# Dealing a modulation's partial sums out between weight splits, and joining the sample's statistics in one matmul

## Chip, cores and metric

One core of a Trainium2 chip runs the whole program. The metric is device time in microseconds: the median of 3 runs, beside one profiled execution, from which every duration below is taken. Engines: TensorE (PE), VectorE (DVE), ScalarE (ACT), GpSimd (POOL), and SyncE (SP), whose queue issues the loads of the weights.

## What is computed

One layer of a streaming encoder, in fp32, for 256 prompt and 32 sample tokens (288 columns) of width 2048:

```python
mod = jax.nn.silu(c) @ w_ada + b_ada
sh1, sc1, g1, sh2, sc2, g2 = [t[:, None, :] for t in jnp.split(mod, 6, axis=-1)]
u = layer_norm(x) * (1 + sc1) + sh1
t, pool_state, C, n, m = token_mixer(u, ...)
x = layer_norm(ALPHA * x + g1 * t, ln1_g, ln1_b)
u = layer_norm(x) * (1 + sc2) + sh2
f = (jax.nn.silu(u @ w_gate) * (u @ w_up)) @ w_down
x = layer_norm(ALPHA * x + g2 * f, ln2_g, ln2_b)
```

`token_mixer` projects u by w_in (2048 x 13328), pools one part over windows, runs 8 heads of mLSTM attention with carried state on another, and merges both by w_pa, w_pb and w_out. `mod` has six parts of 2048, for prompt and sample: j = 0 and 1 feed the first norm, j = 2 to 5 (the later modulation) are needed after w_out.

## The kernel before

All weights are streamed once, in units of 512 KB (128 x 1024 fp32). TensorE multiplies in a split form: the weight is cast to a high part on ACT (L97), the rest of it is taken on DVE as a low part (L98), and each k-tile and block of 128 columns takes three products of 288 columns: hi x hi (L199), hi x lo of the activations (L200), lo of the weight x hi (L201). A full unit makes 24 such matmuls. There are 579 weight units and 192 units of w_ada; the latter are "plain", with no split. 64 of these go to TensorE (parts 0 and 1), and 128 to DVE: the later modulation consists of 16 sums (j, c), each over 8 units, and `ada_dve` issues four steps for a unit (two k-tiles by prompt and sample, L335 and L337), each adding 128 x 512 scaled weights to `aacc`. After the eighth unit a small background task (`ada_sum`) joins the partitions with 8 matmuls, adds the bias and sets `modF`.

The class `Weights` sets the order of the streaming. `_loads` (L79 to L87) issues loads on SP into a ring of `RAW_BUFS = 6` buffers: up to six units ahead of `done`, the oldest plain unit that is converted and not yet used, or else the number of converted units. `_split` issues cast and lo into a ring of four hi/lo pairs. `next` is called as the program takes up a unit; it converts ahead until `depth` weight units are ready (2, then 4), then hands out its own. The program is scheduled by hand: the order in which instructions are written is the order on each engine.

The plan runs: setup and a staged start while parts 0 and 1 of the modulation are made; then groups of 256 output columns, four units each (`group`): w_in for heads 2 to 7, in the order v, o, k, q (24 groups, `rest`), the gates with w_pa and w_pb (`merge`), w_out, then the second norm, w_gate and w_up in pairs, w_down. After each group comes `ada_slot`, which takes as many ada units as a quota has become due: 96 of the 128 in `rest`, merge and w_out by the weights `R`, 32 in gate and up (`ADA_LATE`). Within a group `pump` runs small background tasks: attention for the heads (its instructions are around L930 to L1110), evacuations, parts of the sums.

Sample tokens lie on 4 blocks of 32 partitions (4 blocks of 512 columns); `block_stats` (L425 to L440) joins mean and variance of the blocks with two matmuls by `sel4` and four small DVE instructions, at setup, in `norm_open` (second norm, end) and in `second`.

Of the kernel before, what the change touches and what calls it, by code (L numbers as in the profile page):

```python
# [37 lines left out]
GW = 256  # L38
# [11 lines left out]
class Weights:  # L50
# [3 lines left out]
    def __init__(self, nc, raw_p, cv_p):  # L54
        self.nc, self.raw_p, self.cv_p = nc, raw_p, cv_p
        self.units, self.blocks, self.srcs = [], [], None
        self.raw, self.ready = {}, {}
        self.n_dma = self.n_conv = self.pos = 0
        self.depth = 0

    def add(self, name, k0, nk, c0, ncols):

# [15 lines left out]

    def _loads(self):  # L79
        live = [u for u in range(self.pos, self.n_conv) if self.units[u][1]]  # L80
        done = min(live + [self.n_conv])
        while self.n_dma < min(len(self.units), done + RAW_BUFS):
            shape = self.units[self.n_dma][0]
            t = self.raw_p.tile(shape, F32, tag="raw", name="raw", bufs=RAW_BUFS)
            self.nc.sync.dma_start(out=t, in_=self.srcs[self.n_dma])
            self.raw[self.n_dma] = t
            self.n_dma += 1  # L87

    def _split(self, u):
        shape, plain = self.units[u]  # L90
        raw = self.raw.pop(u)
        if plain:
            self.ready[u] = (raw, None, shape[1])
            return
        hi = self.cv_p.tile(shape, F32R, tag="hi", name="hi", bufs=CONV_BUFS)
        lo = self.cv_p.tile(shape, F32R, tag="lo", name="lo", bufs=CONV_BUFS)
        self.nc.scalar.copy(hi, raw)  # L97
        self.nc.vector.tensor_tensor(lo, raw, hi, op=ALU.subtract)  # L98
        self.ready[u] = (hi, lo, shape[1])

    def next(self, keep=0):

        self.ready.pop(self.pos - 1, None)
        self._loads()
        held = sum(not self.units[u][1] for u in range(self.pos - keep, self.n_conv))
        while self.n_conv < self.n_dma and (held < self.depth or self.units[self.n_conv][1]):
            held += not self.units[self.n_conv][1]
            self._split(self.n_conv)
            self.n_conv += 1
            self._loads()  # L110
        self.pos += 1
        return self.ready[self.pos - 1]
# [3 lines left out]
def tile_stream_layer(  # L116
# [15 lines left out]
    dram = ctx.enter_context(tc.tile_pool(name="spill", bufs=1, space=bass.MemoryType.DRAM))  # L132
    kw_d, v_d = (dram.tile([NH, 128, 2, HD], F32, name=n) for n in ("kwd", "vd"))
    W = Weights(nc, raw_p, cv_p)
    plan, bg, pools, T = [], [], {}, {}

    n_misc = [0]

# [180 lines left out]

    def ada_dve(j, c, q):  # L320

        n = CS // 512

        def run():
            raw = W.next()[0]
            if q == 0:
                while T.get("aacc_busy"):
                    run_task(T["aacc_busy"])
                T["aacc"] = small.tile([128, 2, 512], F32, tag="aacc", name="aacc")
            acc = T["aacc"]  # L330
            for kk in range(n):
                for s in range(2):
                    col = scl[:, n * q + kk, s:s + 1]
                    if q == 0 and kk == 0:
                        nc.vector.tensor_scalar(out=acc[:, s], in0=raw[:, kk], scalar1=col, scalar2=None, op0=ALU.mult)  # L335
                    else:
                        nc.vector.scalar_tensor_tensor(out=acc[:, s], in0=raw[:, kk], scalar=col, in1=acc[:, s],  # L337
                                                       op0=ALU.mult, op1=ALU.add)
            if q == KT // n - 1:
                while T.get("sum"):  # L340
                    run_task(T["sum"])
                T["sum"] = T["aacc_busy"] = later(ada_sum(j, c, acc), 4)

        plain((("w_ada", q * n, n, j * D + c * 512, 512), run))

    def ada_end(j, c, t):
        k0 = 4 * c
# [3 lines left out]
    def ada_sum(j, c, acc):  # L351
        t = misc()
        for g in range(4):
            for s in range(2):
                nc.tensor.matmul(t[32 * g:32 * g + 32, 0:128], lhsT=es[:, s], rhs=acc[:, s, g * 128:(g + 1) * 128],  # L355
                                 start=(s == 0), stop=(s == 1), tile_position=(0, 32 * g))
        T["aacc_busy"] = None
        yield from ada_end(j, c, t)
        T["sum"] = None

    dve_left = [(j, c, q) for j, c in ADA_DVE for q in range(8)]

# [59 lines left out]
        for g in gens:  # L422
            yield from g

    def block_stats(mv):  # L425

        mean, v = mv[:, 0:1], mv[:, 1:2]
        t = misc()
        nc.tensor.matmul(t[:, 0:1], lhsT=sel4, rhs=mean, start=True, stop=True)
        yield 1  # L430
        d = small.tile([128, 2], F32, tag="dmv", name="dmv", bufs=2)
        nc.vector.tensor_tensor(d[:, 0:1], mean, t[:, 0:1], op=ALU.subtract)
        nc.vector.scalar_tensor_tensor(out=d[:, 1:2], in0=d[:, 0:1], scalar=d[:, 0:1], in1=v,
                                       op0=ALU.mult, op1=ALU.add)
        nc.vector.tensor_copy(mean, t[:, 0:1])
        t = misc()
        nc.tensor.matmul(t[:, 0:1], lhsT=sel4, rhs=d[:, 1:2], start=True, stop=True)
        yield 1
        nc.vector.tensor_copy(v, t[:, 0:1])
        yield 1  # L440

    def stat_tiles():
        return (small.tile([128, 3, 2], F32, tag="mv", name="mv", bufs=3),
                small.tile([128, 3], F32, tag="rstd", name="rstd", bufs=3))

    def aggr(sts):


        n = len(sts)
        mv, r = stat_tiles()  # L450
        for i, (st, blocks) in enumerate(sts):
            nc.vector.bn_aggr(out=mv[:, i], in_=st)
            if blocks:
                for _ in block_stats(mv[:, i]):
                    pass
        rsqrt(r[:, 0:n], mv[:, 0:n, 1])
        return [(mv[:, i], r[:, i:i + 1]) for i in range(n)]

    def row_stats(src):
        n = src.shape[1] // 512  # L460
        st = small.tile([128, 4, 6], F32, tag="bst", name="bst", bufs=3)[:, 0:n]
        weave(stat_steps(src, st))
        return st, n == 1

    def stat_steps(src, st):
        for c in range(st.shape[1]):
# [105 lines left out]
    cnt = const.tile([128, 16], F32, name="cnt")  # L572
    nc.gpsimd.iota(cnt, pattern=[[1, 16]], base=1, channel_multiplier=0, allow_small_or_imprecise_dtypes=True)
    nc.vector.reciprocal(out=cnt, in_=cnt)
    sel4 = const.tile([128, 128], F32, name="sel4")
    for b in range(1, 4):
        nc.gpsimd.tensor_tensor(sel4[:, 0:32], ident[:, 0:32] if b == 1 else sel4[:, 0:32],
                                ident[:, b * 32:(b + 1) * 32], op=ALU.add)
    nc.gpsimd.tensor_scalar(out=sel4[:, 0:32], in0=sel4[:, 0:32], scalar1=0.25, scalar2=None, op0=ALU.mult)
    nc.gpsimd.tensor_copy(sel4[:, 32:64], sel4[:, 0:32])  # L580
    nc.gpsimd.tensor_copy(sel4[:, 64:128], sel4[:, 0:64])
    es4 = const.tile([128, 2], F32, name="es4")
    nc.gpsimd.tensor_scalar(out=es4, in0=sel4[:, 0:2], scalar1=4.0, scalar2=None, op0=ALU.mult)
    modF = const.tile([128, 6, 16, 2], F32, name="modF")
    vecF = const.tile([128, 120], F32, name="vecF")
    cn = const.tile([128, 48], F32, name="cn")
# [24 lines left out]
    def setup():  # L611
# [28 lines left out]
        for s in range(2):  # L640
            nc.scalar.activation(out=scl[:, :, s], in_=t[:, 16 * s:16 * s + 16], func=AF.Silu)
        x, (mv, r) = T["x"], stat_tiles()
        for i in range(3):
            nc.vector.bn_aggr(out=mv[:, i], in_=row_stats(x[i])[0])
        nc.vector.tensor_copy(cn, t[:, 0:48])

        def rest():
            bs = block_stats(mv[:, 2])
            for _ in range(3):
                yield next(bs)  # L650
            rsqrt(r, mv[:, :, 1])
            for c in (slice(0, 512), slice(512, D)):
                for i in (2, 0, 1) if c.start == 0 else (0, 1):
# [493 lines left out]
        return f  # L1147

    def out_open():
        close_pool("bh")  # L1150
        close_pool("ua")
        p = open_pool("xr", "left")
# [38 lines left out]
    def norm_open(fill):  # L1191

        drain()
        mv, r = T["stat"] = stat_tiles()
        bs = block_stats(mv[:, 2])
        first = chain(*[affine(i, 0, mv, r) for i in range(3)])
        nc.vector.bn_aggr(out=mv[:, 2], in_=T["st"][2])
        next(bs)
        for i in range(2):
            nc.vector.bn_aggr(out=mv[:, i], in_=T["st"][i])  # L1200
        for _ in range(2):
            next(fill, None)
            next(first)
            next(bs)
        weave(rsqrt_steps(r, mv[:, :, 1]), first, fill)

    def second_open():
        T["states"] = state_steps()
        norm_open(every(F[0], islice(T["states"], F[1])))
        close_pool("mg")  # L1210
# [5 lines left out]
    def second():  # L1216
# [21 lines left out]
        def early():  # L1238
# [5 lines left out]
            for c in cs:  # L1244
                norm(0, c)

        weave(chain(affine(0, 1, mv, r), stats(0)), every(F[2], islice(fill, 8 - F[1])),
              chain(affine(2, 1, mv, r), stats(2), block_stats(mv2[:, 2])))
        weave(chain(affine(1, 1, mv, r), stats(1)), twice(early()), every(F[3], fill))
        rsqrt(r2[:, 1:2], mv2[:, 1:2, 1])  # L1250
        sample_columns(T["xs"], xh[2])
# [60 lines left out]
        return keep if part == 0 else res_evac(j, 5, last) if part == NPART - 1 else more  # L1312

    def fin_open():
        close_pool("u2")
        p = open_pool("ln2", "left")
        T["gb"] = row_tiles(p, ("g2", "b2"))
# [29 lines left out]
    merge += [(x, j) for j in range(1, D // GW) for x in "ab "[j == 1:]]  # L1347
    n_ada, n1, n2 = [0], len(dve_left) - ADA_LATE, len(dve_left)
    late = [w for x, j in merge for w in R[1 + (j > 1)][x]] + [R[3]] * (D // GW - 2) + [0, 0]
    quota = chain(shares(n1, [R[0]] * len(rest) + late), (n1 + n for n in shares(n2 - n1, [1] * (2 * (DFF // GW) - 4) + [0] * 4)))  # L1350
    for u in ada_first(0):
        plain(u)
        do(lambda: next(T["setup"]))
# [56 lines left out]
            group("w_down", f0, FPT, j * GW, GW, "act", down_evac(part, j))  # L1410
    do(finish)
    W.bind(pack)
    for step in plan:
        step()

# [48 lines left out]
```

## Time and profile before

| what | us |
|---|---|
| median of 3 runs (lowest, highest) | 2040.82 (2037.26, 2042.93) |
| profiled execution | 2038.8 |
| its span | 2036.9 |
| PE busy | 1972.4 |
| DVE busy | 1381.4 |
| ACT busy | 772.8 |

How to read it: an engine's busy time is the sum of what it worked on, the span runs from the first to the last instruction. A timeline row gives start, duration, engine, line, operation, result <- operands, shape, number of instructions, and in brackets how long the engine had been idle and who released it. A row of waits gives engine, line, who is waited for, us in total, times, the longest. A row of the windows gives the stretch and its length, then each engine's busy time with instructions in it, the granted clock of TensorE (1.00 is full), the share of time of the DMA engines and GB/s. A row of DMA issues gives result <- source, queue, number, KB, and the median us from issue to landing.

### The profile page before, as it was taken

Reading aid. Unit: us, or ns where it says so; the run is one execution under the profiler, and the core shown is the slowest. Engines: PE = TensorE matmul, PEld = TensorE weight load, DVE = VectorE, ACT = ScalarE, POOL = GpSimd, SP = SyncE. Lnnn points to the kernel's source line nnn. Section 1 sums busy time; section 2 is a strip of 40 time slices with the busy share of each in tenths; the row PEclk is TensorE's granted clock in tenths of the full one; section 3 lists DMA queues with packets and bytes.
Section 4 is the critical chain, followed back from the end, with each engine's and each line's share of the span. In section 5 each row is a group of like instructions: output and inputs, shape, how many; then the busy total and the mean of one; then the engine's idle time right before and its main releaser. Section 6 shows DMA issues by size and latency. Waiting matters only on the chain.

```text
span 2036.9 us, 36604 instructions
## 1 busy us (share of the span) xinstructions
PE 1972.4 (97%) x14952; PEld 1898.4 (93%) x14952; DVE 1381.4 (68%) x2341; ACT 772.8 (38%) x1106; POOL 75.1 (4%) x132
## 2 busy tenths in 40 slices
PE   6999999999999999999999899999999999999995
PEld 5788889999999999999999799999999999999995
DVE  6777787888798568877787765656544565565555
ACT  3333444343433433333334453333333333333331
POOL 1000022000001000000000100000000000001000
PEclk9999999999999999999999899999999999999998
DMA  8878657666666557767797356556555566666541
GB/s 288 280 267 269 198 187 225 209 231 210 213 217 214 160 187 237 238 223 234 231 330 252 126 170 196 195 192 207 180 171 167 189 195 195 196 197 209 180 157 61
DMA packets 126040, 421.85 MB, mean 207 GB/s; under 512 B 14302, under 2 KB 23238, under 8 KB 125104
## 3 DMA queue, kind: packets, MB, share of 16 engines
q1 hardware_dynamic: 118320, 405.59, 61.2%
q0 software_dynamic: 2976, 9.18, 1.5%
q10 hardware_dynamic: 4576, 4.74, 0.7%
q8 instruction: 117, 1.92, 0.4%
q14 instruction: 51, 0.42, 0.1%
HBM read 408.57 MB, written 10.89 MB: 206 GB/s over the span
## 4 chain that ended last, share of the span: by engine, by line
PE 88%; DVE 7%; ACT 2%; DMA 2%; issue 1%; DVEq 0%; ACTq 0%
PE acc L199 28%; PE acc L200 27%; PE acc L201 27%; DVE lo L98 2%; DMA raw<-in_w_in_dram 1%; PE ada L303 1%; DVE aacc L337 1%; ACT hi L97 1%; PE m L539 1%; PE m L1040 1%; DVE xt L1187 0%; DVE xt L1184 0%; PE m L355 0%; PE m L1071 0%; DVE pf L706 0%
## 5 line engine op out<-in xcount | busy, mean ns | idle before, releaser
L98 DVE TENSOR_TENSOR lo<-raw,hi 128x1024 fp32r<-128x1024 f32 (+2 forms) x579 | 680.6, 1185 | 492.5 <-ACT hi L97 490.7
L97 ACT CAST hi<-raw 128x1024 fp32r<-128x1024 f32 (+2 forms) x579 | 585.0, 1015 | 753.6 <-PE acc L200 485.0
L199 PE MATMUL acc<-uhi,hi 128*128 128x288 f32 x1680 | 510.3, 304 | 10.1 <-ACT hi L97 5.2
L201 PE MATMUL acc<-uhi,lo 128*128 128x288 f32 x1680 | 497.3, 296 | 6.7 <-DVE lo L98 6.7
L200 PE MATMUL acc<-ulo,hi 128*128 128x288 f32 x1680 | 498.5, 297 | 0.0
L199 PE MATMUL acc<-vhi,hi 128*128 128x288 f32 x1408 | 418.0, 297 | 0.8 <-ACT vhi L474 0.8
L200 PE MATMUL acc<-vlo,hi 128*128 128x288 f32 x1408 | 416.7, 296 | 0.2 <-DVE vlo L475 0.2
L201 PE MATMUL acc<-vhi,lo 128*128 128x288 f32 x1408 | 416.6, 296 | 0.0
L199 PEld LDWEIGHTS acc<-uhi,hi 128*128 128x128 f32 x1680 | 317.8, 189 | 41.3 <-issue 25.2
L337 DVE SCALAR_TENSOR_TENSOR aacc<-raw,scl,aacc 128x512 f32<-128x512 f32 x480 | 328.1, 750 | 0.0
L201 PEld LDWEIGHTS acc<-uhi,lo 128*128 128x128 f32 x1680 | 317.2, 189 | 8.0 <-DVE lo L98 7.8
L200 PEld LDWEIGHTS acc<-ulo,hi 128*128 128x128 f32 x1680 | 317.6, 189 | 0.2
L199 PEld LDWEIGHTS acc<-vhi,hi 128*128 128x128 f32 x1408 | 266.0, 189 | 2.2 <-ACT vhi L474 1.4
L200 PEld LDWEIGHTS acc<-vlo,hi 128*128 128x128 f32 x1408 | 264.9, 188 | 0.7 <-DVE vlo L475 0.6
L201 PEld LDWEIGHTS acc<-vhi,lo 128*128 128x128 f32 x1408 | 265.4, 188 | 0.0
L199 PE MATMUL acc<-acthi,hi 128*128 128x288 f32 x704 | 208.2, 296 | 0.0
L201 PE MATMUL acc<-acthi,lo 128*128 128x288 f32 x704 | 207.8, 295 | 0.0
L200 PE MATMUL acc<-actlo,hi 128*128 128x288 f32 x704 | 207.7, 295 | 0.0
L199 PEld LDWEIGHTS acc<-acthi,hi 128*128 128x128 f32 x704 | 132.4, 188 | 0.2 <-issue 0.2
L201 PEld LDWEIGHTS acc<-acthi,lo 128*128 128x128 f32 x704 | 132.2, 188 | 0.0
L200 PEld LDWEIGHTS acc<-actlo,hi 128*128 128x128 f32 x704 | 132.1, 188 | 0.0
L200 PE MATMUL acc<-blo,hi 128*128 128x288 f32 x256 | 75.9, 296 | 1.1 <-DVE blo L475 1.1
(307 smaller groups left out, 1924.4 us busy)
## 6 DMA issues: line engine op xcount, KB each, us to landing
raw<-in_w_in_dram SPq DMA_DIRECT2D x202, 512.0 KB, 4.4
raw<-in_w_ada_dram SPq DMA_DIRECT2D x192, 512.0 KB, 4.4
raw<-in_w_gate_dram SPq DMA_DIRECT2D x88, 512.0 KB, 4.3
raw<-in_w_up_dram SPq DMA_DIRECT2D x88, 512.0 KB, 3.8
raw<-in_w_down_dram SPq DMA_DIRECT2D x80, 512.0 KB, 3.5
raw<-in_w_pb_dram SPq DMA_DIRECT2D x32, 512.0 KB, 4.5
raw<-in_w_out_dram SPq DMA_DIRECT2D x32, 512.0 KB, 5.4
raw<-in_w_pa_dram SPq DMA_DIRECT2D x16, 512.0 KB, 4.4
```

The lines of the kernel that those rows point to most:

```text
L97: self.nc.scalar.copy(hi, raw)
L98: self.nc.vector.tensor_tensor(lo, raw, hi, op=ALU.subtract)
L199: nc.tensor.matmul(o, lhsT=hi[:, kk, c], rhs=xh[:, k], start=first, stop=False)
L200: nc.tensor.matmul(o, lhsT=hi[:, kk, c], rhs=xl[:, k], start=False, stop=False)
L201: nc.tensor.matmul(o, lhsT=lo[:, kk, c], rhs=xh[:, k], start=False, stop=last)
L303: nc.tensor.matmul(t[q:q + 32, j * w:j * w + w], lhsT=scl[:, r0 + i, :], rhs=raw[:, i], start=(r0 + i < 4), stop=(r0 + i >= KT - 4), tile_ ...
L337: nc.vector.scalar_tensor_tensor(out=acc[:, s], in0=raw[:, kk], scalar=col, in1=acc[:, s], op0=ALU.mult, op1=ALU.add)
L539: nc.tensor.transpose(dst, full[:, t0:t0 + n], ident)
L1040: nc.tensor.matmul(t[0:n, c:c + b - a], lhsT=k[:, dt, s0:s0 + n], rhs=q[:, dt, a:b], start=(dt == 0), stop=(dt == 1))
```

## The change

1. `ada_dve` no longer issues its four steps when its unit is taken up. It queues them in `steps`, and `deal` issues two (more if over eight would stay) after each split (`W.between`). The unit stays in `W.held` until its last step; `_loads` counts six units from the oldest held one. If a unit is taken up that has no load yet, `next` deals until it has. `parts_done` issues all that is left and runs the sums' tasks, at the start of w_out, of the second norm, and of the last w_down.
2. The quota of the first six groups of `rest` falls from 1.9 to 0.8; the other groups get the rest.
3. `join` replaces `block_stats`: the blocks' raw statistics are spread with a mask (`block`) in one DVE multiply, brought to all blocks by one matmul (`same`) and aggregated once.

```diff
     def _loads(self):
         live = [u for u in range(self.pos, self.n_conv) if self.units[u][1]]
-        done = min(live + [self.n_conv])
+        done = min([*live, *self.held, self.n_conv])
         while self.n_dma < min(len(self.units), done + RAW_BUFS):
...
         self.nc.vector.tensor_tensor(lo, raw, hi, op=ALU.subtract)
         self.ready[u] = (hi, lo, shape[1])
+        self.between()
 
     def next(self, keep=0):
 
         self.ready.pop(self.pos - 1, None)
         self._loads()
+        while self.n_dma <= self.pos:
+            self.between()
+            self._loads()
...
+            if (kk, s) != (n - 1, 1):
+                return
+            W.held.discard(u)
             if q == KT // n - 1:
...
         def run():
             raw = W.next()[0]
+            W.held.add(W.pos - 1)
+            for kk in range(n):
+                for s in range(2):
+                    steps.append((raw, W.pos - 1, kk, s, step))
+
         plain((("w_ada", q * n, n, j * D + c * 512, 512), run))
+
+    def deal(n=2):
+
+        for _ in range(min(len(steps), max(n, len(steps) - 8))):
+            *a, step = steps.pop(0)
+            step(*a)
...
+    def parts_done(*js):
+
+        deal(len(steps))
+        while any((j, c) not in T.get("parts", ()) for j in js for c in range(4)):
+            run_task(T["sum"])
...
-    def block_stats(mv):
-
-        mean, v = mv[:, 0:1], mv[:, 1:2]
+    def join(mv, st):
+
+
+        w = st.shape[1] * 6
+        flat = small.tile([128, 2 * NT], F32, tag="tmp", name="join", bufs=TMP_BUFS)[:, 0:4 * w]
+        e = flat.rearrange("p (b c) -> p b c", b=4)
+        nc.vector.tensor_tensor(e, st.rearrange("p (o n) c -> p o (n c)", o=1).to_broadcast([128, 4, w]),
+                                block.rearrange("p (b o) -> p b o", o=1).to_broadcast([128, 4, w]), op=ALU.mult)
         t = misc()
-        nc.tensor.matmul(t[:, 0:1], lhsT=sel4, rhs=mean, start=True, stop=True)
+        nc.tensor.matmul(t[:, 0:4 * w], lhsT=same, rhs=flat, start=True, stop=True)
         yield 1
...
+        nc.vector.bn_aggr(out=mv, in_=t[:, 0:4 * w].rearrange("p (n c) -> p n c", c=6))
         yield 1
...
-    quota = chain(shares(n1, [R[0]] * len(rest) + late), (n1 + n for n in shares(n2 - n1, [1] * (2 * (DFF // GW) - 4) + [0] * 4)))
+    quota = chain(shares(n1, [0.8] * 6 + [R[0]] * (len(rest) - 6) + late), (n1 + n for n in shares(n2 - n1, [1] * (2 * (DFF // GW) - 4) + [0] * 4)))
...
     W.bind(pack)
+    W.between = deal
```

The line numbers move: casts L97 are now L99, lo L98 is L100, the products are L205 to L207, the steps L338 and L340, copies L938 are L946, the state's update L982 is L990.

First place: ACT, in groups of the heads (`pf` are copies of a group's result out of PSUM; `eo`, `kw`, `vT`, `dd` and `b` belong to attention). Before:

```order
L938 COPY pf<-acc 128x288 x2
L97 CAST hi<-raw 128x1024
L1074 COPY dd<-m 32x257
L97 CAST hi<-raw 128x1024 x2
L963 ACTIVATE eo<-m 128x512
L964 ACTIVATE eo<-m 32x256
L97 CAST hi<-raw 128x1024
L974 ACTIVATE kw<-m,wst 128x256 x2
```

Now:

```order
L946 COPY pf<-acc 128x288 x2
L99 CAST hi<-raw 128x1024 x4
L982 ACTIVATE kw<-m,wst 128x256 x2
L982 ACTIVATE kw<-m,wst 32x256
L983 DMA kwd<-kw 128x512
L946 COPY pf<-acc 128x288 x2
L99 CAST hi<-raw 128x1024
L275 COPY adarow<-m 128x128
L99 CAST hi<-raw 128x1024 x3
```

Casts that stood one by one between the attention's instructions now stand in a row behind the copies of the group before.

Second place: DVE, in the same groups (`co` is the state's update from a matmul, `hh` the norm of a head's result). Before:

```order
L471 TENSOR_SCALAR hh<-hh,hmv,hrr 32x256
L98 TENSOR_TENSOR lo<-raw,hi 128x1024 x3
L337 SCALAR_TENSOR_TENSOR aacc<-raw,scl,aacc 128x512 x8
L98 TENSOR_TENSOR lo<-raw,hi 128x1024
L982 SCALAR_TENSOR_TENSOR co<-c_5116,dec,m 128x257 x2
L98 TENSOR_TENSOR lo<-raw,hi 128x1024 x3
L337 SCALAR_TENSOR_TENSOR aacc<-raw,scl,aacc 128x512 x8
```

Now:

```order
L990 SCALAR_TENSOR_TENSOR co<-c_5031,dec,m 128x257 x2
L340 SCALAR_TENSOR_TENSOR aacc<-raw,scl,aacc 128x512 x4
L287 TENSOR_TENSOR modF<-m,vecF 128x4 x2
L289 TENSOR_SCALAR modF<-modF 128x8
L100 TENSOR_TENSOR lo<-raw,hi 128x1024
L338 TENSOR_SCALAR aacc<-raw,scl 128x512 x2
L100 TENSOR_TENSOR lo<-raw,hi 128x1024
L340 SCALAR_TENSOR_TENSOR aacc<-raw,scl,aacc 128x512 x2
L100 TENSOR_TENSOR lo<-raw,hi 128x1024 x2
```

The block of eight steps is gone. The last four steps of a unit, which free its buffer, and the four lo parts of the group that PE takes up next all stand behind the state's update of the group before.

## Rows read from the trace of the kernel before

**Rows 1.** Span and mean granted clock of the core

```profile
core 0: 2036.9 us, clock 0.987
```

**Rows 2.** Busy time of each engine, share of the span, instructions

```profile
PE 1972.4 (97%) x14952; PEld 1898.4 (93%) x14952; DVE 1381.4 (68%) x2341; ACT 772.8 (38%) x1106; POOL 75.1 (4%) x132
```

**Rows 3.** Waits of PE

```profile
PE acc L201 <- DVE lo L98: 6.7, 5, 4.4
...
PE m L200 <- DVE ylo L475: 2.8, 1, 2.8
...
PE m L437 <- DVE dmv L433: 0.9, 1, 0.9
```

**Rows 4.** Timeline of PE around the gap at 291

```profile
291.00 0.29 PE L200 MATMUL acc<-ulo,hi 128*128 128x288 f32 x1
295.68 0.40 PE L201 MATMUL acc<-uhi,lo 128*128 128x288 f32 x1 [4.38 <-DVE lo L98]
```

**Rows 5.** Timeline of DVE in the same place

```profile
287.16 7.33 DVE L337 SCALAR_TENSOR_TENSOR aacc<-raw,scl,aacc 128x512 f32<-128x512 f32 x8
294.42 2.35 DVE L98 TENSOR_TENSOR lo<-raw,hi 128x1024 fp32r<-128x1024 f32 x2
```

**Rows 6.** Windows: one of rows 9, two behind gaps, one without a gap

```profile
core 0: us, PE busy (x) PEld busy (x) DVE busy (x) ACT busy (x) POOL busy (x), PEclk, DMA share, GB/s
201.50:210.19 8.69, 8.28 (x73) 6.77 (x65) 5.54 (x15) 2.36 (x3) 0.00 (x0) 1.00 0.89 336
295.68:299.50 3.82, 3.82 (x18) 3.82 (x19) 3.69 (x8) 1.11 (x2) 0.00 (x0) 0.58 0.83 295
326.60:329.00 2.40, 2.12 (x9) 2.12 (x10) 2.40 (x5) 0.13 (x1) 0.50 (x1) 0.58 0.65 213
1200.00:1250.00 50.00, 50.00 (x379) 50.00 (x378) 29.97 (x36) 19.29 (x24) 0.00 (x0) 1.00 0.60 186
```

**Rows 7.** DMA issues of the weights

```profile
raw<-in_w_in_dram SPq DMA_DIRECT2D x202, 512.0 KB, 4.4
...
raw<-in_w_down_dram SPq DMA_DIRECT2D x80, 512.0 KB, 3.5
...
raw<-in_w_out_dram SPq DMA_DIRECT2D x32, 512.0 KB, 5.4
```

**Rows 8.** Groups of lo and cast: busy us, mean ns of one, idle before, releaser

```profile
L98 DVE TENSOR_TENSOR lo<-raw,hi 128x1024 fp32r<-128x1024 f32 (+2 forms) x579 | 680.6, 1185 | 492.5 <-ACT hi L97 490.7
L97 ACT CAST hi<-raw 128x1024 fp32r<-128x1024 f32 (+2 forms) x579 | 585.0, 1015 | 753.6 <-PE acc L200 485.0
```

**Rows 9.** The critical chain from 195 to 215: start, us, what

```profile
200.89 0.61 PE ada L303 x8
201.52 5.71 DMA raw<-in_w_in_dram
...
207.30 1.06 ACT hi L97
...
208.39 1.23 DVE lo L98
```

**Rows 10.** Waits of SP's queue on the steps

```profile
SPq L85 <- DVE aacc L337: 255.7, 113, 4.3
```

**Rows 11.** Timeline of DVE in a group of the heads

```profile
421.86 5.38 DVE L337 SCALAR_TENSOR_TENSOR aacc<-raw,scl,aacc 128x512 f32<-128x512 f32 x8
...
445.19 0.88 DVE L982 SCALAR_TENSOR_TENSOR co<-c,dec,m 128x257 f32<-128x257 f32 x2
```

**Rows 12.** Timeline of DVE at an evacuation of up

```profile
1189.59 0.46 DVE L1293 TENSOR_TENSOR sg<-sg,acc 128x288 f32<-128x288 f32 x1 [1.57 <-PE acc L201]
...
1192.82 3.50 DVE L98 TENSOR_TENSOR lo<-raw,hi 128x1024 fp32r<-128x1024 f32 x3 [0.49 <-ACT hi L97]
```

**Rows 13.** Timeline of ACT at copies of a group's result

```profile
435.53 0.70 ACT L938 COPY pf<-acc 128x288 f32<-128x288 f32 x2
```

**Rows 14.** Timeline of DVE at the last norm

```profile
2018.26 0.22 DVE L433 SCALAR_TENSOR_TENSOR dmv<-dmv,mv 128x1 f32<-128x1 f32 x1
```

More of the change, by code (lines that the diff above doesn't have):

```diff
@@ L59, in __init__ @@
         self.depth = 0
+        self.held = set()
+        self.between = lambda: None
     def add(self, name, k0, nk, c0, ncols):
@@ L134, in tile_stream_layer @@
     W = Weights(nc, raw_p, cv_p)
-    plan, bg, pools, T = [], [], {}, {}
+    plan, bg, pools, T, steps = [], [], {}, {}, []
     n_misc = [0]
@@ L322, in ada_dve, with step @@
         n = CS // 512
-        def run():
-            raw = W.next()[0]
-            if q == 0:
+        def step(raw, u, kk, s):
+            if q == kk == s == 0:
                 while T.get("aacc_busy"):
@@ L329, in run @@
                 T["aacc"] = small.tile([128, 2, 512], F32, tag="aacc", name="aacc")
[L330 to L338, printed above, removed]
+            acc, col = T["aacc"], scl[:, n * q + kk, s:s + 1]
+            if q == 0 and kk == 0:
+                nc.vector.tensor_scalar(out=acc[:, s], in0=raw[:, kk], scalar1=col, scalar2=None, op0=ALU.mult)
+            else:
+                nc.vector.scalar_tensor_tensor(out=acc[:, s], in0=raw[:, kk], scalar=col, in1=acc[:, s],
+                                               op0=ALU.mult, op1=ALU.add)
+            if (kk, s) != (n - 1, 1):
+                return
+            W.held.discard(u)
             if q == KT // n - 1:
@@ L342, in run @@
                 T["sum"] = T["aacc_busy"] = later(ada_sum(j, c, acc), 4)
+        def run():
+            raw = W.next()[0]
+            W.held.add(W.pos - 1)
+            for kk in range(n):
+                for s in range(2):
+                    steps.append((raw, W.pos - 1, kk, s, step))
         plain((("w_ada", q * n, n, j * D + c * 512, 512), run))
+    def deal(n=2):
+        for _ in range(min(len(steps), max(n, len(steps) - 8))):
+            *a, step = steps.pop(0)
+            step(*a)
     def ada_end(j, c, t):
@@ L359, in ada_sum @@
         T["sum"] = None
+        T["parts"] = T.get("parts", frozenset()) | {(j, c)}
+    def parts_done(*js):
+        deal(len(steps))
+        while any((j, c) not in T.get("parts", ()) for j in js for c in range(4)):
+            run_task(T["sum"])
     dve_left = [(j, c, q) for j, c in ADA_DVE for q in range(8)]
@@ L423, in chain @@
             yield from g
-    def block_stats(mv):
-        mean, v = mv[:, 0:1], mv[:, 1:2]
+    def join(mv, st):
[4 more added lines that the diff above has]
+                                block.rearrange("p (b o) -> p b o", o=1).to_broadcast([128, 4, w]), op=ALU.mult)
         t = misc()
-        nc.tensor.matmul(t[:, 0:1], lhsT=sel4, rhs=mean, start=True, stop=True)
+        nc.tensor.matmul(t[:, 0:4 * w], lhsT=same, rhs=flat, start=True, stop=True)
         yield 1
[L431 to L439, printed above, removed]
+        nc.vector.bn_aggr(out=mv, in_=t[:, 0:4 * w].rearrange("p (n c) -> p n c", c=6))
         yield 1
@@ L444, in stat_tiles @@
                 small.tile([128, 3], F32, tag="rstd", name="rstd", bufs=3))
[L446 to L457, printed above, removed]
     def row_stats(src):
@@ L462, in row_stats @@
         weave(stat_steps(src, st))
-        return st, n == 1
+        return st
     def stat_steps(src, st):
@@ L574, in tile_stream_layer @@
     nc.vector.reciprocal(out=cnt, in_=cnt)
-    sel4 = const.tile([128, 128], F32, name="sel4")
+    same = const.tile([128, 128], F32, name="same")
     for b in range(1, 4):
-        nc.gpsimd.tensor_tensor(sel4[:, 0:32], ident[:, 0:32] if b == 1 else sel4[:, 0:32],
+        nc.gpsimd.tensor_tensor(same[:, 0:32], ident[:, 0:32] if b == 1 else same[:, 0:32],
                                 ident[:, b * 32:(b + 1) * 32], op=ALU.add)
[L579 to L583, printed above, removed]
+    nc.gpsimd.tensor_copy(same[:, 32:64], same[:, 0:32])
+    nc.gpsimd.tensor_copy(same[:, 64:128], same[:, 0:64])
+    es4 = same[:, 0:2]
+    block = const.tile([128, 4], F32, name="block")
+    nc.vector.tensor_reduce(block, ident.rearrange("p (b c) -> p b c", b=4), axis=mybir.AxisListType.X, op=ALU.add)
     modF = const.tile([128, 6, 16, 2], F32, name="modF")
@@ L642, in setup @@
         x, (mv, r) = T["x"], stat_tiles()
-        for i in range(3):
-            nc.vector.bn_aggr(out=mv[:, i], in_=row_stats(x[i])[0])
-        nc.vector.tensor_copy(cn, t[:, 0:48])
+        for i in range(2):
+            nc.vector.bn_aggr(out=mv[:, i], in_=row_stats(x[i]))
         def rest():
-            bs = block_stats(mv[:, 2])
-            for _ in range(3):
-                yield next(bs)
+            yield from join(mv[:, 2], row_stats(x[2]))
+            nc.vector.tensor_copy(cn, t[:, 0:48])
             rsqrt(r, mv[:, :, 1])
@@ L1149, in out_open @@
     def out_open():
+        parts_done(2)
         close_pool("bh")
@@ L1194, in norm_open @@
         mv, r = T["stat"] = stat_tiles()
-        bs = block_stats(mv[:, 2])
+        bs = join(mv[:, 2], T["st"][2])
         first = chain(*[affine(i, 0, mv, r) for i in range(3)])
-        nc.vector.bn_aggr(out=mv[:, 2], in_=T["st"][2])
         next(bs)
@@ L1200, in norm_open @@
             nc.vector.bn_aggr(out=mv[:, i], in_=T["st"][i])
[L1201 to L1204, printed above, removed]
+        next(fill, None)
+        next(first)
+        next(bs)
         weave(rsqrt_steps(r, mv[:, :, 1]), first, fill)
     def second_open():
+        parts_done(3, 4)
         T["states"] = state_steps()
@@ L1247, in second @@
         weave(chain(affine(0, 1, mv, r), stats(0)), every(F[2], islice(fill, 8 - F[1])),
-              chain(affine(2, 1, mv, r), stats(2), block_stats(mv2[:, 2])))
+              chain(affine(2, 1, mv, r), stat_steps(x[2], st[2]), join(mv2[:, 2], st[2])))
         weave(chain(affine(1, 1, mv, r), stats(1)), twice(early()), every(F[3], fill))
@@ L1314, in fin_open @@
     def fin_open():
+        parts_done(5)
         close_pool("u2")
```

## Prediction, before the change had run

> **What bounds the kernel now.** I read the spans first: one core, 2036.9 us at a mean granted clock of 0.987 [rows 1]; the profiled execution takes 2038.8 us with what lies around the span. Then the busy times: PE 97% with 14952 matmuls, DVE 68%, ACT 38% [rows 2]. So TensorE sets the time almost everywhere, and a change costs or gains what it does to PE's gaps. The waits of PE show how few there are: on the low parts (L201 <- DVE lo) 6.7 us in 5 waits, one of them 4.4; on ylo 2.8 [rows 3]. The large one stands in the timeline at 291.0: the next matmul starts at 295.68 after 4.38 us of waiting for lo [rows 4]. DVE's timeline tells why: eight steps of the later modulation (L337) hold DVE for 7.33 us from 287.16, and the two splits behind them end at 296.8 [rows 5]. After that gap the windows show the clock: 18 matmuls in 3.82 us at a granted 0.58, the lower of its two levels (1.2 GHz), where a stretch with no gap does 379 in 50 us at 1.00 (2.4 GHz), 0.132 us each [rows 6]. 18 would take 2.38 us at that rate, so the gap costs a further 1.44 us.
>
> One weight unit is 24 matmuls, 3.17 us of PE. To be ready it needs a load, a cast on ACT and a lo on DVE: 4.4 us in the median from issue to landing for w_in (3.5 for w_down, 5.4 for w_out) [rows 7], then 1.02 and 1.19 us [rows 8]. That chain of 6.6 us is hidden only because it starts two or more units ahead. One place of before shows it bare on the critical chain: DMA 5.71, cast 1.06, lo 1.23, and then the first product, from 201.52 to 210.19 [rows 9]; PE had other matmuls for that time, 73 in 8.69 us [rows 6].
>
> **The change, part by part.**
>
> *Dealing out.* 128 ada units of the later sums issue the same 512 steps as before, two of them behind each split, so DVE's work is unchanged. What changes is when a raw buffer comes free. A unit is `held` until its last step, loads stop six units behind the oldest held one, and steps are dealt only by a split, which needs a loaded unit. With an ada unit ahead of a group of four weight units and another one or two behind it, the splits ahead run out while the first still has steps queued. Nothing then deals until PE's program reaches a unit that has no load: the new loop in `next` deals there. The order shows it (the second place above): four steps, then a split, two steps, a split, all behind the state's update L990 of the group that PE has just been given. On SP's queue the ada load waits for those steps, and the weight loads queue behind it; before, that wait came to 255.7 us on 113 loads without reaching PE [rows 10], since the loads ran 5 to 9 units ahead.
>
> Counted over the program: of 579 weight units, before 505 are split three units ahead of their products and only the first with none between. In the change 64 more have load *and* split behind the last product of the weight unit directly before: 24 in the groups of w_in for heads 2 to 7, 18 in the merge, 6 in w_out, 16 in gate and up. For each, PE runs dry until the chain is through. I sort them by the last instruction on DVE, ahead of the freeing steps, that waits for a matmul.
>
> - A, 27 places: it waits for the unit just finished (the state's update, the evacuation of up). DVE's work on it lies between 0.88 us (two L982) [rows 11] and 2.74 (1189.59 to the start of the splits at 1192.82, less 0.49 for a cast) [rows 12]; I take 1.8, the middle. Four steps: eight take 5.38 us [rows 11], so 2.7. Load 4.4, cast 1.02, lo 1.19. Together 11.1, less 0.6 that PE still has to do, like the eight small matmuls in [rows 9]: 10.5 us, 284 in all. Ends: 8.7 with 0.88 and a load of 3.5; 13.0 with 2.74 and 5.4 and nothing beside it.
> - B, 20 places: that instruction lies one or two units back, so the chain has a start of 1.5 x 3.17 = 4.75: 5.75 us, 115 in all. Ends 2.4 and 9.8.
> - C, 17 places: DVE freed the buffer long before; what is left is ACT's order, since the casts stand behind the copies out of the group's PSUM (first place above). Copies 0.70 [rows 13], cast 1.02, lo 1.19, less 0.6: 2.3 us, 39 in all; up to 2.9 with no cover.
>
> In 22 of the 64 places one or two ada loads, 25 in all, stand in the queue ahead of the weight's. At the 295 GB/s of [rows 6] a 512 KB unit takes 1.8 us, so between 0 (the 4.4 is already that of a busy queue) and 45 us; I take 22. The clock: each of 64 gaps is followed by a stretch at the low level, as after the gaps of 4.38 and 2.81 us in before (both 0.58) [rows 6]; 64 x 1.44 = 92, with 0 as the lower end, since the small gaps of C may not cost it.
>
> *What it gives back.* The gap at 291 is of the kind that dealing takes away: 4.4 + 1.44; so may be the one of 2.8 + 1.44, behind the same eight-step blocks: 10 us in all, 0 as the other end. `parts_done` moves the last sum's small work in front of the norm at three places; a few instructions of 0.2 to 0.7 us like [rows 14].
>
> *The join.* Two matmuls and four small DVE instructions become one multiply, one matmul and one aggregate. PE waited 0.9 us once for the second matmul's input [rows 3], and one of its instructions took 0.22 [rows 14]: some 0.5 to 1 us at each of two open places. At setup PE is fed by loads, so nothing. Less what `parts_done` puts there (0.75 for one step of that size), I take 2 us of gain; ends -1 and 3. The smaller quota of ada units in six groups moves them later and is in the count of 64.
>
> Sum: 2038.8 + 284 + 115 + 39 + 22 + 92 - 12 = 2578.8; **2579 us**. The median of the runs shown is 0.1% above the profiled execution, which changes nothing at this size. With all ends low, 27 x 8.7 + 20 x 2.4 + 17 x 2.3 - 13, no queue and no clock: 2348. With all high, 27 x 13 + 20 x 9.8 + 17 x 2.9 + 45 + 92 + 1: 2773.
>
> **Rivals.**
>
> *Faster: the loads run ahead all the same.* If DVE and SP get through the queued work while PE is still on earlier units, only the gains are left: 2038.8 - 12 = 2027. For it: DVE is 68% busy and the worst gap of PE came from a block of eight steps. Against it: the four steps come behind instructions that wait for the group's matmuls, and no idle time lets DVE overtake its own order. It decides if all 64 places are such that PE has over 6.6 us of other work. The Trainium skill says the same as this rival (Perfetto Trace Analysis, Optimizing Scalar/DVE Operations): where Scalar or Vector are not saturated but cause bubbles on other engines, breaking up instructions may let work end sooner. By that rule the time would fall to 2027; the gap of 4.38 us agrees with its premise, and the order of DVE speaks against its conclusion here. Chance 0.05.
>
> *Mildly slower: only the casts are late.* If the dealt steps reach DVE early at nearly all places, loads land in time and the 64 gaps are those of C: 64 x 2.3 + 92 - 12 = 2266. For it: DVE has 655 us of idle time in before. Against it: in 47 of 64 places the instruction ahead of the steps waits for a recent matmul. Chance 0.15.
>
> *Much slower: the units behind are late too.* 121 more units are split just one unit ahead (64 before). Where their load is issued no earlier either, 6.6 - 3.2 = 3.4 us is missing. For half of them 60 x 3.4 = 204 on top: 2783. Against it: they come in the same burst as a unit with a gap, and the gap covers them. Chance 0.10.
>
> The forecast has 0.70.
>
> **How the numbers follow.** A measurement can tell about 0.3%, 6 us, from no change. Faster by more: the first rival but for a small part, 0.04; within: 0.02; slower: 0.94. The range takes the forecast with its bounds, from 2300, a little below its low end and part of the way to the mild rival, to 2800, which takes in the third; outside lie the rest of the mild rival (0.13) and the first.
>
> **What would show it.** Right: PE busy near 80% of a span near 2577, some 60 waits of PE's L205 to L207 on casts and lo of 3 to 11 us, their chains leading from lo over cast and DMA to an aacc step; a mean granted clock clearly under 0.987 in 230 to 1900 us; SP's waits on aacc much over 255.7 us. Wrong: waits of PE still under 10 us a line, which is the first rival; or 64 waits of 2 to 3 us on casts with landed loads, the mild one. If the waits are there but far shorter than 10.5 in class A, the mis-sized term is DVE's or the load's.

## The result, and the profile after

The changed kernel takes 2365.58 us in the median (2364.55 to 2368.54, 4 runs) where before takes 2040.34 beside it: a ratio of 1.1597, 95% interval 1.1577 to 1.1617. It is slower by 325 us. The direction and the range were right; the forecast of 2579 put the loss at 540 us and so was 1.7 times too large.

Span and mean granted clock (0.987 before, [rows 1]):

```profile
core 0: 2366.8 us, clock 0.932
```

From the page of the changed kernel: busy times [rows 2], the clock granted in 40 slices, and the median landing of a load of w_in [rows 7].

```profile
PE 2092.7 (88%) x14944; PEld 1993.8 (84%) x14944; DVE 1378.1 (58%) x2330; ACT 761.8 (32%) x1106; POOL 64.5 (3%) x130
...
PEclk9999999898888998998899889999999999899998
...
raw<-in_w_in_dram SPq DMA_DIRECT2D x202, 512.0 KB, 4.6
```

PE's share falls from 97% to 88%, yet its busy time rises by 120.3 us with eight matmuls fewer: the same work at a lower clock, 0.932 in the mean. Not all of this is clock: with PE's busy time weighted by the clock granted in it, 101.7 us of the rise go to the lower clock; the other 18.6 come with 149 separate stretches of work where before has 43. The loads land about as fast as before (4.6 against 4.4). Where PE waits, the waits tell, first of the changed kernel, then the row on casts of before that stands beside [rows 3]:

```profile
PE acc L207 <- DVE lo L100: 110.3, 58, 6.3
PE acc L205 <- ACT hi L99: 104.8, 57, 3.9
PE m L374 <- DVE aacc L340: 9.2, 2, 5.3
PE m L460 <- DVE join L457: 7.8, 3, 2.9
```

```profile
PE acc L199 <- ACT hi L97: 5.2, 8, 1.9
```

These are 58 waits on lo parts and 57 on casts, 215.1 us where before had 6.7 + 5.2. The difference, 203.2, and the 120.3 of busy time make 323.5 of the 329.9 us by which the span grew; two waits of the sums' own matmuls (L374) for the dealt steps add 9.2, and all other waits are 2.8 us shorter. Counted along PE's timeline behind 250 us, waits over 0.6 us on casts (L99) and lo parts (L100) that lie less than 9 us apart taken together, there are 53 places with 206.5 us, 3.9 us each: the order had shown 64. So the places are there; what one costs is less than I forecast.

A place of class A, behind the evacuation of up, on four engines. PE first; a unit's first matmul needs the cast, the third needs lo:

```profile
1571.59 0.29 PE L207 MATMUL acc<-vhi,lo 128*128 128x288 f32 x1
1574.76 0.61 PE L205 MATMUL acc<-vhi,hi 128*128 128x288 f32 x1 [2.88 <-ACT hi L99]
1575.17 0.44 PE L206 MATMUL acc<-vlo,hi 128*128 128x288 f32 x1
1578.09 0.61 PE L207 MATMUL acc<-vhi,lo 128*128 128x288 f32 x1 [2.48 <-DVE lo L100]
```

ACT:

```profile
1573.33 0.43 ACT L484 CAST acthi<-sg 128x288 fp32r<-128x288 f32 x1 [0.89 <-DVE sg L1301]
1573.67 3.88 ACT L99 CAST hi<-raw 128x1024 fp32r<-128x1024 f32 x4
```

DVE:

```profile
1571.52 0.45 DVE L1301 TENSOR_TENSOR sg<-sg,acc 128x288 f32<-128x288 f32 x1 [9.69 <-PE acc L207]
...
1573.79 0.46 DVE L485 TENSOR_TENSOR actlo<-sg,acthi 128x288 fp32r<-128x288 f32 x1 [0.50 <-ACT acthi L484]
1574.17 2.73 DVE L340 SCALAR_TENSOR_TENSOR aacc<-raw,scl,aacc 128x512 f32<-128x512 f32 x4
1576.82 1.22 DVE L100 TENSOR_TENSOR lo<-raw,hi 128x1024 fp32r<-128x1024 f32 x1
```

and the issues of loads on SP's queue, whose durations of merged rows run from the first to the last:

```profile
1551.95 10.23 SPq L87 DMA_DIRECT2D raw<-in_w_gate_dram  x4
1576.93 0.33 SPq L87 DMA_DIRECT2D raw<-in_w_ada_dram  x1
```

PE ends at about 1571.9. ACT finishes the evacuation and casts at once, from 1573.67: the load was there, there is no idle time in front of it. DVE runs the evacuation, the four steps (2.73), then lo, from 1576.82, while the cast is done beside the steps. PE waits 2.88 + 2.48 = 5.36 us; I had 10.5 for this class. SP shows what I had wrong: the four gate loads that belong to the next group were issued from 1551.95 on, over 10 us before the steps that I took to free their buffers. Only the ada load behind them, at 1576.93, waited for those steps.

The dearest places stand in the merge, at 928, 987 and 1165 us, with 9.0 to 9.3 us each. There eight steps still stand in a row in front of lo (in the whole trace eleven such blocks are left, so the block of eight is not gone everywhere). PE, then DVE:

```profile
928.04 0.40 PE L205 MATMUL acc<-uhi,hi 128*128 128x288 f32 x1 [3.87 <-ACT hi L99]
934.03 0.61 PE L207 MATMUL acc<-uhi,lo 128*128 128x288 f32 x1 [5.45 <-DVE lo L100]
```

```profile
927.45 5.38 DVE L340 SCALAR_TENSOR_TENSOR aacc<-raw,scl,aacc 128x512 f32<-128x512 f32 x8
932.75 1.22 DVE L100 TENSOR_TENSOR lo<-raw,hi 128x1024 fp32r<-128x1024 f32 x1
```

A place of class C, behind the evacuation of gate: PE, then DVE.

```profile
1944.60 0.29 PE L207 MATMUL acc<-vhi,lo 128*128 128x288 f32 x1
1946.32 0.40 PE L205 MATMUL acc<-vhi,hi 128*128 128x288 f32 x1 [1.44 <-ACT hi L99]
...
1947.58 0.40 PE L207 MATMUL acc<-vhi,lo 128*128 128x288 f32 x1 [0.73 <-DVE lo L100]
```

```profile
1936.15 2.73 DVE L340 SCALAR_TENSOR_TENSOR aacc<-raw,scl,aacc 128x512 f32<-128x512 f32 x4
1946.30 1.22 DVE L100 TENSOR_TENSOR lo<-raw,hi 128x1024 fp32r<-128x1024 f32 x1 [7.41 <-ACT hi L99]
```

Here the steps ran ten microseconds ahead, and copies, cast and lo remain: 1.44 + 0.73 = 2.17 us, where I had 2.3. What follows such a place differs: the windows from the first matmul on give a granted clock (third number from the end) of 0.50, the lower level, behind the A place, and of 1.00 behind this C place, but 0.71 behind another. Of the eight places behind gate two show 1.00 and six 0.69 to 0.73; the eight behind up show 0.50 to 0.61 (windows of 5.5 to 7.3 us).

```profile
1574.76:1582.00 7.24, 4.76 (x18) 4.41 (x19) 7.24 (x11) 2.79 (x3) 0.00 (x0) 0.50 0.51 157
1946.32:1952.00 5.68, 4.95 (x35) 4.72 (x36) 5.68 (x7) 3.72 (x4) 0.00 (x0) 1.00 0.44 129
1974.50:1980.00 5.50, 4.77 (x23) 4.54 (x24) 5.50 (x7) 2.79 (x3) 0.00 (x0) 0.71 0.47 128
```

### The profile page after: what moved, and what is told of

Its sections match the earlier page's. It is cut to its first block, busy times and chain, and to the rows that moved or that the text cites. A ratio compares the mean times of both kernels' runs of the same rounds, so it can differ in the third digit from the quotient of the medians.

```text
span 2366.8 us, 36608 instructions
## 1 busy us (share of the span) xinstructions
PE 2092.7 (88%) x14944; PEld 1993.8 (84%) x14944; DVE 1378.1 (58%) x2330; ACT 761.8 (32%) x1106; POOL 64.5 (3%) x130
## 5 line engine op out<-in xcount | busy, mean ns | idle before, releaser
L100 DVE TENSOR_TENSOR lo<-raw,hi 128x1024 fp32r<-128x1024 f32 (+2 forms) x579 | 676.6, 1181 | 550.9 <-ACT hi L99 546.2
L99 ACT CAST hi<-raw 128x1024 fp32r<-128x1024 f32 (+2 forms) x579 | 572.2, 1014 | 658.8 <-PE acc L206 380.7
L207 PE MATMUL acc<-uhi,lo 128*128 128x288 f32 x1680 | 522.8, 311 | 68.1 <-DVE lo L100 68.1
L205 PE MATMUL acc<-uhi,hi 128*128 128x288 f32 x1680 | 533.3, 317 | 54.7 <-ACT hi L99 50.2
L206 PE MATMUL acc<-ulo,hi 128*128 128x288 f32 x1680 | 517.3, 308 | 0.0
L205 PE MATMUL acc<-vhi,hi 128*128 128x288 f32 x1408 | 430.0, 305 | 32.6 <-ACT hi L99 31.6
L207 PE MATMUL acc<-vhi,lo 128*128 128x288 f32 x1408 | 427.4, 304 | 21.7 <-DVE lo L100 21.7
L206 PE MATMUL acc<-vlo,hi 128*128 128x288 f32 x1408 | 427.8, 304 | 0.4 <-DVE vlo L485 0.4
L205 PEld LDWEIGHTS acc<-uhi,hi 128*128 128x128 f32 x1680 | 337.7, 201 | 90.4 <-ACT hi L99 63.1
L207 PEld LDWEIGHTS acc<-uhi,lo 128*128 128x128 f32 x1680 | 337.7, 201 | 75.5 <-DVE lo L100 75.5
L206 PEld LDWEIGHTS acc<-ulo,hi 128*128 128x128 f32 x1680 | 337.3, 201 | 0.1
L340 DVE SCALAR_TENSOR_TENSOR aacc<-raw,scl,aacc 128x512 f32<-128x512 f32 x480 | 333.4, 747 | 0.0
L205 PEld LDWEIGHTS acc<-vhi,hi 128*128 128x128 f32 x1408 | 275.7, 196 | 37.3 <-ACT hi L99 35.2
L207 PEld LDWEIGHTS acc<-vhi,lo 128*128 128x128 f32 x1408 | 275.5, 196 | 25.8 <-DVE lo L100 25.8
L205 PE MATMUL acc<-acthi,hi 128*128 128x288 f32 x704 | 209.0, 297 | 2.9 <-ACT hi L99 2.9
L207 PE MATMUL acc<-acthi,lo 128*128 128x288 f32 x704 | 208.6, 296 | 2.5 <-DVE lo L100 2.5
L205 PEld LDWEIGHTS acc<-acthi,hi 128*128 128x128 f32 x704 | 133.1, 189 | 3.3 <-ACT hi L99 3.1
L207 PEld LDWEIGHTS acc<-acthi,lo 128*128 128x128 f32 x704 | 132.8, 189 | 2.8 <-DVE lo L100 2.8
L205 PE MATMUL acc<-mghi,hi 128*128 128x288 f32 x256 | 81.8, 319 | 11.2 <-ACT hi L99 11.2
```

The source lines that it names most:

```text
L205: nc.tensor.matmul(o, lhsT=hi[:, kk, c], rhs=xh[:, k], start=first, stop=False)
L206: nc.tensor.matmul(o, lhsT=hi[:, kk, c], rhs=xl[:, k], start=False, stop=False)
L207: nc.tensor.matmul(o, lhsT=lo[:, kk, c], rhs=xh[:, k], start=False, stop=last)
```

## Experiments

Theory 1: the cost lies in the places with no unit split ahead, where PE must wait for copies, cast, steps and lo, and in the clock behind them. Rivals: the steps between the splits delay lo wherever they stand; late loads; the quota or the forced end of the sums. Times are medians, ratios are against before on the same chip (median 2039.8 to 2040.3).

**Restoring the look-ahead.** In `next`, after the conversion loop, which now repeats:

```diff
+            if held >= self.depth or not self.held:
+                break
+            self.between()
+            self._loads()
```

Expected: 

> The change as it is, but steps are also dealt as soon as no further unit can be split ahead, so that splits run three units ahead of their products again (504 of 579, as before). Theory 1 (the 64 places where casts and lo parts stand behind the group just finished are the whole cost): the gaps go and the time is 2025 to 2040 us. Theory 2 (two steps between splits delay lo parts wherever they stand, or the fewer units loaded ahead cost): most of the cost stays, over 2150 us.

Measured 2031.09 us, ratio 0.9954 (0.9941 to 0.9966). The places are gone:

```profile
PE acc L210 <- ACT hi L99: 5.4, 8, 1.8
...
PE acc L212 <- DVE lo L100: 2.6, 3, 1.4
```

The quota, the forced ends and the join are still in it, so none of these is the cause; the kernel is even 9 us faster than before. The result is what theory 1 expects, but it does not rule out that steps between splits are at fault, for the early deals undo most of the dealing: in DVE's order 500 of the 512 steps stand in runs of four or eight again, as all do in before, and 12 in pairs, where the change has 236 in pairs. On the pairs the trace of the change itself tells more: 134 lo parts follow a step with no idle time between, and PE waited over 0.6 us for 29 of them, all in the places counted above. No run keeps the steps in pairs and the look-ahead too.

**Steps at once.** `run` deals all it has queued; the rest of the change stays.

```diff
+            deal(len(steps))
```

Expected: 

> The change, but each unit's four steps are issued at once, as before it; join, quota and the forced end of the sums stay. Theory 1: nothing of the cost is in those parts, 2035 to 2042 us, the gap of 4.4 us at about 291 still there or moved. Theory 2 (the quota or the forced ends carry part of it): over 2060 us.

Measured 2030.39 us, ratio 0.9949 (0.9937 to 0.9962), under the range that I gave theory 1, since the gap at 291 is gone; the quota's run below tells why. The cost comes from queueing the steps alone, and the gain of 9 us does not come from dealing.

**The join alone**, in the kernel before.

Expected: 

> The kernel before with the join of the statistics alone. By my prediction 2 us less than before (2038 to 2040 us); by the tail of the changed kernel's trace, where the stretch from the last evacuation to the scaling is 0.15 us shorter, no difference that can be measured, 2039 to 2041 us.

Measured 2039.94 us, ratio 0.9997 (0.9988 to 1.0006): nothing that can be measured. The value lies in both of my ranges, so it does not decide between them.

**No unit ahead, without dealing.** In the kernel before, splits stop at a unit of the modulation that has not been taken up (`_stop` gives its number):

```diff
-        while self.n_conv < self.n_dma and (held < self.depth or self.units[self.n_conv][1]):
+        stop = self._stop()
+        while self.n_conv < min(self.n_dma, stop) and (held < self.depth or self.units[self.n_conv][1]):
```

Expected: 

> The kernel before with blocks of four steps at once and loads as far ahead as ever, but splits never run past a unit of the modulation that has not been taken up: 88 places with no unit split ahead (the change has 64), the lo parts ahead of the steps there. Theory 1: each place costs 2.2 to 3 us of waits (copies, cast, lo) and 1 to 2 us of lower clock: 2320 to 2480 us, with no wait of a cast on a load there. Theory 2 (late loads or the steps in front of lo are needed for the cost): under 2150 us.

Measured 2428.34 us, ratio 1.1892 (1.1874 to 1.1911), inside the range of theory 1. PE's waits and the busy times:

```profile
PE acc L208 <- ACT hi L97: 168.4, 85, 3.9
PE acc L210 <- DVE lo L98: 70.2, 89, 2.3
```

```profile
PE 2137.3 (88%) x14952; PEld 2025.5 (83%) x14952; DVE 1372.5 (57%) x2341; ACT 750.9 (31%) x1106; POOL 68.5 (3%) x132
```

With no dealt step in front of lo, casts carry most of it (168.4 us) and no wait on lo is over 2.3. The 88 places cost 238.6 us of waits, less the 11.9 of before 2.6 each, and the busy time of PE is 164.9 us over that of before, 1.9 per place. The change gives 1.9 as well by the 64 places of the order (120.3 / 64), but 2.3 by the 53 of its trace, where the same count finds 87 places in this run. Of the casts that PE waited for over 0.6 us behind 250 us, each had its load landed 6.7 us or more before it began, and no steps stand directly in front of the lo parts that PE waited for so long: the missing look-ahead is enough.

**Where the quota stands.** The first run's kernel with the old quota, then the kernel before with the new one alone.

```diff
-    quota = chain(shares(n1, [R[0]] * len(rest) + late), ...
+    quota = chain(shares(n1, [0.8] * 6 + [R[0]] * (len(rest) - 6) + late), ...
```

Expected: 

> The dealing with early deals as in the first run, but the old quota (1.9 in the first six groups). If dealing itself takes the gaps at 291 and 324 away: 2027 to 2033 us, like that run. If the smaller quota gave the gain: 2036 to 2041 us, with a wait on lo left near 290 us.

Expected: 

> The kernel before with the smaller quota alone (0.8 in the first six groups), steps in blocks as before. If the quota gave the gain: 2028 to 2033 us, with no wait over 2 us of PE between 270 and 340 us. If dealing or the forced ends did: 2037 to 2042 us.

Measured 2037.16 us, ratio 0.9981 (0.9972 to 0.9991), and 2034.61 us, ratio 0.9970 (0.9959 to 0.9980). With the old quota the eight steps at the gap of 4.38 us at 291 [rows 4] run as four and four with a lo part between, and of the gap 1.19 us are left:

```profile
293.01 0.40 PE L212 MATMUL acc<-uhi,lo 128*128 128x288 f32 x1 [0.86 <-DVE lo L100]
...
296.80 0.40 PE L212 MATMUL acc<-uhi,lo 128*128 128x288 f32 x1 [0.33 <-DVE lo L100]
```

A wait stands at 313.67 where before has none:

```profile
313.67 0.40 PE L212 MATMUL acc<-uhi,lo 128*128 128x288 f32 x1 [2.89 <-DVE lo L100]
```

0.86 + 0.33 + 2.89 is 4.08, against 4.38 and the 2.8 on ylo [rows 3], which is gone. The quota takes all of it away: from 250 to 400 us PE is busy all the time, where before has 142.08 of 150. Windows of the quota's run and of before:

```profile
250.00:400.00 150.00, 150.00 (x1129) 145.19 (x1127) 120.61 (x211) 65.53 (x109) 27.84 (x30) 1.00 0.65 206
```

```profile
250.00:400.00 150.00, 142.08 (x1048) 137.28 (x1047) 123.64 (x219) 61.55 (x103) 25.11 (x26) 0.98 0.66 205
```

The first run met the case in which the quota gave the gain; the second lies between its two cases. So the quota gives 6 of the 9 us, the rest of the change with its look-ahead restored some 3 to 4. The intervals of the quota's run and of the steps-at-once run only just overlap, so how the last 3 us divide stays open.

**Buffers as I had assumed them.** The change, then before, with unit n always in raw buffer n mod 6:

```diff
-            t = self.raw_p.tile(shape, F32, tag="raw", name="raw", bufs=RAW_BUFS)
+            t = self.raw_p.tile(shape, F32, tag=f"raw{self.n_dma % RAW_BUFS}", name="raw", bufs=1)
```

Expected: 

> The change with six raw buffers of their own, unit n always in buffer n mod 6, so that the first load past a held unit has to take that unit's buffer, as my prediction assumed. If that assumption is what made it too slow: 2480 to 2640 us, with waits of casts on loads at the gaps. If the sizes were wrong elsewhere: 2350 to 2400 us as the change.

Expected: 

> Control to the run ahead of this: the kernel before with the same fixed buffers. Its loads run 5 to 9 units ahead, so no more than a few us either way: 2035 to 2055 us.

Measured 2615.09 us, ratio 1.2818 (1.2793 to 1.2844), and 2281.78 us, ratio 1.1186 (1.1169 to 1.1204). The first is what was expected of my assumption, and a place in it has my chain of class A. PE, DVE, ACT, SP:

```profile
590.21 0.61 PE L205 MATMUL acc<-uhi,hi 128*128 128x288 f32 x1 [9.60 <-ACT hi L99]
...
591.47 0.61 PE L207 MATMUL acc<-uhi,lo 128*128 128x288 f32 x1 [0.41 <-DVE lo L100]
```

```profile
580.63 0.88 DVE L990 SCALAR_TENSOR_TENSOR co<-c,dec,m 128x257 f32<-128x257 f32 x2 [4.68 <-issue]
581.42 2.73 DVE L340 SCALAR_TENSOR_TENSOR aacc<-raw,scl,aacc 128x512 f32<-128x512 f32 x4
590.19 1.23 DVE L100 TENSOR_TENSOR lo<-raw,hi 128x1024 fp32r<-128x1024 f32 x1 [6.04 <-ACT hi L99]
```

```profile
589.11 1.04 ACT L99 CAST hi<-raw 128x1024 fp32r<-128x1024 f32 x1 [9.13 <-DMA raw<-in_w_in_dram]
```

```profile
567.29 17.22 SPq L87 DMA_DIRECT2D raw<-in_w_ada_dram  x2
584.60 1.87 SPq L87 DMA_DIRECT2D raw<-in_w_in_dram  x4
```

State's update 0.88, steps 2.73 to 584.15, the ada load and the four of w_in issued at once behind them, 4.5 us later the cast, then lo: PE waits 9.60 + 0.41 = 10.0 us, against 10.5 forecast. But the control missed its range by far: before, too, loses 241 us when its loads may not pass a buffer that steps still hold.

```profile
SPq L85 <- DVE aacc L337: 1127.0, 113, 17.6
```

That wait was 255.7 us before [rows 10]. So 2615 against 2366 is not the cost of this assumption at the 64 places alone; the fixed order of buffers is bad for both kernels, which lie 333 us apart with it and 325 without. What it shows is the mechanism and the size of the chain where the load does wait: with loads and casts counted off in order, 52 of the 67 casts that PE waited for over 0.6 us behind 250 us began within 0.3 us of their load's landing.

**How far ahead is enough.** The first run's early deals, but only below one unit ahead, and below two:

```diff
-            if held >= self.depth or not self.held:
+            if held >= 2 or held >= self.depth or not self.held:
```

(3 in place of 2 for two units; `held` counts the unit that is taken up.)

Expected: 

> The first run's early deals, but only when no unit at all is split ahead: one unit of look-ahead is kept (159 places with one, none with none). One unit of PE work is 3.17 us; a place with the dealt steps behind an evacuation takes about 2.9 to 5.4 us in the change, one with copies, cast and lo alone 2.2. If what is left is that minus 3.17: 2035 to 2080 us. If a place costs the same wherever one unit only is ahead: over 2250 us.

Expected: 

> The same with two units of look-ahead kept (109 places with two where before had three): 6.3 us cover every place, so the time is that of the first run, 2028 to 2036 us. If look-ahead of three is needed: over 2040 us.

Measured 2108.63 us, ratio 1.0341 (1.0326 to 1.0357), and 2042.55 us, ratio 1.0016 (1.0006 to 1.0027). PE's waits of the first, and of the second:

```profile
PE acc L212 <- DVE lo L100: 50.1, 28, 5.0
...
PE acc L210 <- ACT hi L99: 5.7, 10, 1.8
```

```profile
PE acc L212 <- DVE lo L100: 10.8, 9, 2.5
```

One unit of 3.17 us hides every cast but not the steps and lo behind an evacuation: 28 waits, up to 5.0 us, 1.8 in the mean. I had left the clock behind them out, hence more than 2080: PE is busy for 28.0 us longer than with three units ahead (1996.0 against 1968.0). With two units nine small waits remain, and 11 us more than with three: two do not quite cover it, and my expectation of 2028 to 2036 was missed too. The less is kept ahead, the more steps stand in pairs (6 pairs with three units, 23 with two, 39 with one), so the series does not vary the look-ahead alone.

## Why the prediction was right or wrong

**What bounds the kernel** was right: PE, by its gaps. All of the loss is waits of PE and its longer busy time behind them.

**The mechanism** was right: in the places that the order shows, casts and lo parts stand behind the group just finished. Taking these places away gives the time back (2031), making them without any dealing gives the loss (2428).

**Class A, 10.5 us for 27 places**, is the step that failed. It said that the ada load waits for the steps and the weight loads queue behind it. The trace shows the weight loads issued before the steps, and the ada load behind them, at the A place above: a load that is *written* behind a step does not have to *wait* for it. Of 45 waits on casts over 0.6 us behind 250 us, none has ACT idle for a DMA in front of the cast, and with loads and casts counted off in order each cast's load had landed at least 1.3 us before, half of them more than 12. That a buffer which is free for longer goes to the next load is my explanation; no trace names the buffer that a load takes, but tying it to the unit's number brings the late loads about. The sign that I had named for them, SP's waits on the steps, came without them, at 636.6 us against 255.7:

```profile
SPq L87 <- DVE aacc L340: 636.6, 127, 18.8
```

The 4.4 us of the load go out of the sum. So does the cast, which runs on ACT beside the steps on DVE; I had added two chains that lie side by side. 10.5 - 4.4 - 1.02 = 5.1, and the eight places behind up show 4.8 to 5.4.

**Class B, 5.75 us for 20 places**: without load and cast its remainder is 0.3 us. I did not match the places of the trace to the classes; those with a wait on lo alone cost 0.96 to 6.26 us. **Class C** was right, 2.17 against 2.3. With 5.1, 2.3 and 2.3 the sum of the classes is 27 x 5.1 + 37 x 2.3 = 223, fitted after the fact; measured were 203 of waits, and 9 at L374.

**The queue in front of the weight loads, 22 us**: nothing, as no cast waits there.

**The clock, 92 us**, was too small: the busy time behind the gaps grew by 120.3, 101.7 of it at the lower clock. I took one low stretch per gap from two single gaps of before. Most places in the change have two, one for the cast and one for lo, with two matmuls between. It is uneven: 0.50 for 7.24 us behind an A place, none behind two C places of eight.

**What it gives back, 10 us**: in the change nothing of it can be seen; in the kernels with the look-ahead restored it is 9, most of it by the quota, which I had priced at nothing. With the old quota 4.08 us of waits were left of the 7.2 that I had credited to dealing. **The join, 2 us**: none measured, but the interval, -2.4 to +1.2 us (0.9988 to 1.0006 of 2040), does not exclude it.

**The total** is right in part by luck: waits and queue were forecast at 460 us and measured at 212, the clock was a quarter too small, which made up for some of it, and the range was 500 us wide; 2366 lies close to its low end.

**The rivals.** The truth lies nearest the mild one: loads in time at all places, as it said, but at 29 waits lo stands behind other work of DVE, the steps above all (89.9 us), which it did not have, and its price of 1.44 for the clock was too low: hence 2366 and not 2266. The Trainium skill's rule (Perfetto Trace Analysis, Optimizing Scalar/DVE Operations), that breaking up instructions may let work end sooner, is not borne out by the change. In the kernel with the look-ahead restored and the old quota one place agrees: the eight steps at 291 run in two parts, and the wait falls from 4.38 to 1.19 us. The 3.2 us that this kernel gains hold other parts of the change too. So breaking the block up can help at a place, as long as nothing that must be early is made to wait for the pieces.

## What to carry to other kernels

When work is queued to be dealt out "between" other work, ask what happens when the other work runs out: here dealing needed splits, splits needed loads, loads needed dealing, and the look-ahead that hid casts fell to none in 64 places by the order, at some 3 us of waits and 2 us of longer PE time each. Price a stall engine by engine from the order, adding only what one engine does in sequence, and read from the trace which instruction a load really waits for before putting its latency into the sum. A change that mixes four edits can hide a gain: the smaller quota alone was worth 6 us.

## What the runs showed that I had not expected

With every raw buffer tied to its unit's number, the kernel before loses 12% (2281.78 us), with the very same instructions in the same order on every engine: SP's waits on the steps grow from 255.7 to 1127.0 us. So the freedom to hand out another buffer is worth 241 us here; what the depth of the ring is worth no run tested.
